# A one-core two-block transformer kernel: the order of work around its norms, its start and its attention heads

## The chip, the core and the metric

The kernel runs on one core of one Trainium2 chip. Its engines are TensorE (PE), VectorE (DVE), ScalarE (ACT), GpSimd (POOL) and SyncE (SP), which issues most of the DMAs. The metric is the device time of one execution in microseconds, as the median of several runs.

## The reference, cut to what matters

One sequence of T = 256 tokens of width 1024 passes through two blocks, all in fp32.

```python
# first block
xn = rmsnorm(x, norm1_g)
h = x + token_mixers(xn)           # w_in (1024 x 7168), RG-LRU scan, convolutions, gates, w_out
t = rmsnorm(h, norm2_g)
q = t @ w_q                        # PEER: 8 heads, two halves of 128 keys each, top 16 of 256 sums
h = h + sum(gate * gelu(u[idx] . t) * v[idx])    # 16384 experts; u and v are 16384 x 1024
x2 = rmsnorm(h, final_g)
# second block, layer 0: differential attention; layer 1: forgetting attention
for i in (0, 1):
    y = attention_i(h)             # 8 differential or 16 forgetting heads
    h = layer_norm(ALPHA * h + y)
    gate, up = split(h @ ffn_w_in) # 2816 each
    f = (silu(conv3(gate)) * up) @ ffn_w_out
    h = layer_norm(ALPHA * h + f)
```

The kernel does not gather experts. It multiplies every token with all 16384 rows of u and of v, and the gates are zero where an expert was not chosen.

## The kernel before, in words

**Products.** TensorE multiplies in a form that takes an fp32 operand rounded to fewer bits. So each operand is split in a high part and a low rest, and each product is made of three (`mm3`, L206 to L209; `add_part`, L231 to L237): high by high, low by high, high by low. Two layouts occur. `proj` gives features by tokens (128x256, 24 products for one weight tile of 128 output features); `add_part` gives tokens by features (128x512), and adds over many weight tiles into four PSUM banks `acc`, one for each pair of token half `tt` and column half `nh`. Four further banks, tag `w`, are handed out by `bank` in turn.

**Weights.** `attn_order` and `ffn_order` write down the order of all weight tiles, 512 KB each. `w_dma` issues their loads on SP's queue into `raw`, `w_split` makes `whi` on ScalarE (L186) and `wlo` on VectorE (L187). They run ahead of their use by as many tiles as there are buffers.

**Order.** The code is written engine by engine in the order of a program, and a scheduler reorders each engine's instructions by its own estimate. `pin` keeps an instruction in program order, and `paced` and `queued` let an instruction be placed only behind a given other one (for `paced`, the latest weight split).

**Stages.** At the start, x is transposed for the sums of squares of norm1 (`x_turn`, `x_sums`) and the first projections `xa` are made of x times the gain, `xgh` and `xgl`; the norm's factor `rB` is multiplied in afterwards. Then follow the input projections (`vb`, `bb`, `cb`, `gx`, `ga`, `ma`, `mb`), with the recurrence `lru_ops` on VectorE and `tables`, which makes rotary tables and one lambda, and the output product `wo`. `finish` runs the last weight tiles for one quarter of the output after another and calls `after` for each quarter.

**Turns.** Where a norm ends, the tokens-by-features result must be turned to features by tokens. `turned` transposes four 128x128 squares into one bank `tq`, copies the high part out on ScalarE and the rest on VectorE. For norm2 and norm3, `residual` adds the quarter to the residual `hk` (called `Hr` for norm3) on VectorE, multiplies it by the norm's gain (`hg`; for norm3 written into the other half of `Hr`), turns it, and sums squares on ScalarE. For a layer norm, `layer_norm` writes sums `z` and the norm's result into one tile.

**PEER.** `q` projections use norm2's turned result; the choice of the top 16 runs on VectorE while 128 `u` tiles are projected; then 128 `v` tiles are added into `pv`. Behind them the `dpv` products (values) and `dqk` (queries and keys) of differential attention begin with norm3's turned result, `x3h` and `x3l`.

**Attention.** `attention` loops over n from 0 to 7. For each n it projects a query and key tile, and at first one value tile too. `scores` makes a head's scores and softmax, `tp` transposes the probabilities `a` (bank `d1tp` for head 1), `pv_` multiplies them with the values (`do`), and `ot` turns the head's result (`dt`) and splits it into `doh` and `dol`. `wo(m)` adds head m into the output (`dwo`). The last part of `attention` writes the order of the remaining heads by hand.

**FFN.** `ffn` makes for each column c a gate product `fg` and an up product `fu`, a convolution and SiLU `fy` on ScalarE and VectorE, and later the output product `fo`. Four of the up products are made early in the other layout (`ul`) and only transposed in the loop.

Of the kernel before, what the change touches and what calls it, by code (L numbers as in the profile page):

```python
# [21 lines left out]
T = 256  # L22
# [9 lines left out]
NW = 3  # L32
# [3 lines left out]
LEAD = 4  # L36
NEG = -1.0e30
# [20 lines left out]
def kernel(  # L58
# [57 lines left out]
    def attn_order(tag, vt, qk, wo):  # L116
        for k in range(LEAD):
            order.append(((tag + "v", k), vt[k]))
        for n in range(8):
            order.append(((tag + "q", n), qk[n]))  # L120
            order.append(((tag + "k", n), qk[8 + n]))
            if LEAD + n < 8:
                order.append(((tag + "v", LEAD + n), vt[LEAD + n]))
        for n in range(8):
            order.append(((tag + "o", n), wo[n]))

    def ffn_order(i):
        for j in range(4):
            order.append((("fl%d" % i, j), [ff_in[i, NF:NF + 4, :, (2 * j + kk) * 128:(2 * j + kk + 1) * 128]
                                            for kk in range(2)]))  # L130
        for c in range(NF):
            order.append((("fg%d" % i, c), ff_in[i, c]))
            if c >= 4:
                order.append((("fu%d" % i, c), ff_in[i, NF + c]))
# [219 lines left out]
    with tc.tile_pool(name="b1", bufs=1) as b1, tc.tile_pool(name="w1", bufs=1) as w1:  # L354
# [15 lines left out]
        w_dma(4)  # L370
# [10 lines left out]
        def scaled(c):  # L381
            act.activation(xgh[:, c, :], x[:, c, :], AF.Copy, scale=P_("norm1_g", c))
            dve.scalar_tensor_tensor(xgl[:, c, :], x[:, c, :], P_("norm1_g", c), xgh[:, c, :].bitcast(F32),
                                     op0=OP.mult, op1=OP.subtract)
# [16 lines left out]
        x_turn(0)  # L401
        for c in range(2):
            scaled(c)
        w_split(1)
        for c in range(2, 4):
            scaled(c)
        x_turn(1)
        x_sums(0)
        for c in range(4, KC):
            scaled(c)  # L410
        w_split(2)
        x_sums(1)
# [9 lines left out]
        XG = 3  # L422
        pss = {}

        def xa_proj(c):
            W = weight(("in", c))
            pss[c] = bank([128, T], f"xa{c}")
            proj(pss[c], W, xgh, xgl)

        for c in range(XG):  # L430
            xa_proj(c)
# [3 lines left out]
        for c in range(8):  # L435
            if c >= XG:
                xa_proj(c)
            ps = pss.pop(c)
            dve.tensor_tensor(xa[:, c, :], ps, rB, op=OP.mult)
# [4 lines left out]
                                     op0=OP.mult, op1=OP.subtract)  # L444

# [29 lines left out]
        nl = b1.tile([128, 8], F32, name="nlam8")  # L475
        ab = b1.tile([128, 8], F32, name="lamabs")
        zz = b1.tile([128, 8], F32, name="zz")
        dve.tensor_scalar(nl, lamc, -1.0, None, op0=OP.mult)
        dve.tensor_tensor(ab, nl, lamc, op=OP.max)
        act.activation(zz, ab, AF.Exp, scale=-1.0)  # L480
        series_log1p(sp4, zz, [128, 8], b1, "sp")
        dve.scalar_tensor_tensor(sp4, nl, 0.0, sp4, op0=OP.max, op1=OP.add)
        dve.tensor_scalar(sp8, sp4, -8.0, None, op0=OP.mult)
        dve.tensor_scalar(sp4, sp4, 4.0, None, op0=OP.mult)
        dve.tensor_scalar(g8, P_("subln"), 1.0 - LAM_INIT, None, op0=OP.mult)
# [90 lines left out]
        tables()  # L576
# [29 lines left out]
        g2 = full("g2", tag="xch").rearrange("p a b -> p (a b)")[:, 0:D]  # L606
        row_bcast(g2, "norm2_g")
        hg = full("hg", tag="xnh").rearrange("p a b -> p (a b)").rearrange("p (t d) -> p t d", t=2)

        def residual(hk, xk, hg, grow, acc, ss, junk, xh, xl):  # L610


            def after(tt, nh):
                ns = slice(nh * 512, nh * 512 + 512)
# [7 lines left out]
        junk = full("junk2", tag="yb").rearrange("p a b -> p (a b)")[:, 0:512]  # L622
        finish(acc, tail, residual(hk, xk, hg, g2, acc, ss2, junk, hgh, hgl))
        nc.sync.dma_start(hdram, hk.rearrange("p a b -> p (a b)"))
        st["behind"] = []
# [3 lines left out]
    with pctx:  # L629
# [256 lines left out]
        finish(acc, tail, residual(hk, hk, hg, g3, acc, ss3, junk, xh, xl))  # L886
# [6 lines left out]
    with ExitStack() as b2ctx:  # L893
# [15 lines left out]
        def layer_norm(acc, tail, h, li, n, rows_, last=False):  # L909
# [3 lines left out]
            z = tokens("z" + name)  # L913
# [12 lines left out]
            def after(tt, nh):  # L926
                ns, nt = slice(nh * 512, nh * 512 + 512), slice(nh, nh + 1)
                pin(dve.scalar_tensor_tensor(z[:, tt, ns], h[:, tt, ns], ALPHA, acc[2 * tt + nh], op0=OP.mult,
                                             op1=OP.add, accum_out=s[:, tt, nt]))
# [3 lines left out]
                if nh == 0:  # L933
                    return
                t1 = slice(tt, tt + 1)
                pin(dve.tensor_scalar(nm[:, t1], m[:, tt, 0:1], m[:, tt, 1:2], 0.5, op0=OP.add, op1=OP.mult))
                for j in range(2):
                    js = slice(j * 512, j * 512 + 512)
                    pin(dve.scalar_tensor_tensor(z[:, tt, js], z[:, tt, js], nm[:, t1], rows_[0][:, js], op0=OP.add,
                                                 op1=OP.mult))  # L940
                    if j == 0:
# [479 lines left out]
```

## Time and profile before

| What | Value |
|---|---|
| Runs | 1758.74, 1761.19, 1765.67 us; median 1761.19 us |
| Profiled execution | 1761.87 us |
| Its span | 1760.1 us |
| TensorE busy | 1693.4 us (96%) |
| TensorE weight loads busy | 1541.5 us (88%) |
| VectorE busy | 1219.4 us (69%) |
| ScalarE busy | 884.4 us (50%) |
| Chain that ended last | TensorE 79%, VectorE 10%, ScalarE 4% |

The span is what the trace covers; the execution's own time has 1.8 us around it. A high busy share says that an engine is the one to look at, not that it was busy all along at its peak: the rows further down show where it waited, and for what, and at which clock it ran.

### The profile page before, as it was taken

How to read it: one execution, taken by the hardware profiler on the slowest of the kernel's cores; microseconds unless marked ns; L12 is line 12 of the kernel's file. 1: busy time of each engine (PE TensorE's matmuls, PEld its weight loads, DVE VectorE, ACT ScalarE, POOL GpSimd, SP SyncE). 2: the span in 40 equal slices, each digit the busy share in tenths (PEclk: the TensorE clock that was granted, in tenths of full speed). 3: DMA queues.
4: the chain of work that ended last, by engine and by line, in shares of the span. 5: the costliest groups of instructions: out<-in, count | busy, mean ns of one | idle time of the engine just before them, and what ended most of it. 6: DMA issues, size and time to landing. Idle time of an engine off the chain costs nothing.

```text
span 1760.1 us, 30460 instructions
## 1 busy us (share of the span) xinstructions
PE 1693.4 (96%) x11917; PEld 1541.5 (88%) x11917; DVE 1219.4 (69%) x2332; ACT 884.4 (50%) x1498; POOL 128.4 (7%) x104
## 2 busy tenths in 40 slices
PE   7999799999999999999999998988999999999998
PEld 7999699899999999887788886886899979989997
DVE  8868589985477776888855554785766665566665
ACT  6684455444433334445444443564645446555453
POOL 2023010430000000000000000241000000000000
PEclk9999899999999999999999999999999999999999
DMA  7646446455544445446565553741755545347551
GB/s 239 191 158 200 147 144 216 156 176 184 180 156 156 155 156 163 159 159 194 168 216 192 191 192 112 235 132 48 231 188 186 186 147 163 99 134 219 184 186 55
DMA packets 90719, 297.17 MB, mean 169 GB/s; under 512 B 9216, under 2 KB 20560, under 8 KB 89808
## 3 DMA queue, kind: packets, MB, share of 16 engines
q1 hardware_dynamic: 89520, 294.71, 52.0%
q8 instruction: 93, 1.52, 0.4%
q10 hardware_dynamic: 1056, 0.52, 0.1%
q14 instruction: 50, 0.41, 0.1%
HBM read 289.92 MB, written 3.19 MB: 167 GB/s over the span
## 4 chain that ended last, share of the span: by engine, by line
PE 79%; DVE 10%; ACT 4%; issue 2%; DMA 2%; POOL 1%; POOLq 0%; ACTq 0%; SPq 0%; DVEq 0%
PE pv L235 20%; PE ff L235 7%; PE u L207 5%; PE u L208 5%; PE u L209 5%; DVE wlo L187 3%; PE fg L207 2%; PE fg L209 2%; PE fg L208 2%; PE fu L209 2%; PE fu L207 2%; PE fu L208 2%; PE g L815 2%; PE g L816 2%; PE fwo L235 1%
## 5 line engine op out<-in xcount | busy, mean ns | idle before, releaser
L187 DVE TENSOR_TENSOR wlo<-raw,whi 128x1024 fp32r<-128x1024 f32 x384 | 474.9, 1238 | 222.6 <-ACT whi L186 215.7
L186 ACT ACTIVATE whi<-raw 128x1024 fp32r<-128x1024 f32 x384 | 405.5, 1058 | 263.2 <-PE pv L235 118.9
L187 DVE TENSOR_TENSOR W<-raw,W 128x1024 fp32r<-128x1024 f32 x150 | 185.2, 1237 | 124.1 <-ACT W L186 123.7
L208 PE MATMUL u<-xn2h,wlo 128*128 128x256 f32 x928 | 262.8, 283 | 6.0 <-DVE wlo L187 6.0
L207 PE MATMUL u<-xn2h,whi 128*128 128x256 f32 x928 | 264.4, 285 | 0.0
L209 PE MATMUL u<-xn2l,whi 128*128 128x256 f32 x928 | 261.8, 282 | 0.0
L186 ACT ACTIVATE W<-raw 128x1024 fp32r<-128x1024 f32 x150 | 158.4, 1060 | 171.4 <-PE pv L235 67.8
L208 PEld LDWEIGHTS u<-xn2h,wlo 128*128 128x128 f32 x928 | 175.6, 189 | 7.7 <-DVE wlo L187 7.7
L207 PEld LDWEIGHTS u<-xn2h,whi 128*128 128x128 f32 x928 | 176.0, 190 | 0.0
L209 PEld LDWEIGHTS u<-xn2l,whi 128*128 128x128 f32 x928 | 175.4, 189 | 0.0
L835 ACT ACTIVATE H<-u 128x256 f32<-128x256 f32 x128 | 49.2, 384 | 224.4 <-PE u L209 224.4
L235 PE MATMUL pv<-W,ph 128*128 128x512 f32 x416 | 116.3, 391 | 0.0
L235 PE MATMUL pv<-whi,pl 128*128 128x512 f32 x304 | 96.5, 397 | 0.7 <-DVE pl L318 0.7
L235 PE MATMUL pv<-wlo,ph 128*128 128x512 f32 x304 | 95.5, 394 | 0.0
L235 PE MATMUL pv<-whi,ph 128*128 128x512 f32 x304 | 92.3, 402 | 0.0
L235 PEld LDWEIGHTS pv<-W,ph 128*128 128x128 f32 x416 | 77.7, 188 | 16.2
L816 PE MATMUL g<-al,eb 128*128 128x64 f16 x512 | 70.8, 239 | 0.0
L815 PE MATMUL g<-ah,eb 128*128 128x64 f16 x512 | 70.8, 239 | 0.0
L235 PEld LDWEIGHTS pv<-wlo,ph 128*128 128x128 f32 x304 | 57.1, 188 | 13.5
L235 PEld LDWEIGHTS pv<-whi,pl 128*128 128x128 f32 x304 | 56.8, 189 | 13.9 <-DVE pl L318 1.1
L815 PEld LDWEIGHTS <-eb 128*128 128x128 f16 x512 | 56.2, 117 | 11.4 <-issue 6.0
L235 PEld LDWEIGHTS pv<-whi,ph 128*128 128x128 f32 x304 | 55.8, 190 | 10.9
(840 smaller groups left out, 4397.0 us busy)
## 6 DMA issues: line engine op xcount, KB each, us to landing
raw<-in_uT_dram SPq DMA_DIRECT2D x128, 512.0 KB, 3.6
raw<-in_v_dram SPq DMA_DIRECT2D x128, 512.0 KB, 4.2
raw<-in_ff_in_dram SPq DMA_DIRECT2D x80, 512.0 KB, 3.8
raw<-in_w_in_dram SPq DMA_DIRECT2D x56, 512.0 KB, 4.3
raw<-in_ff_out_dram SPq DMA_DIRECT2D x44, 512.0 KB, 3.8
raw<-in_w_q_dram SPq DMA_DIRECT2D x16, 512.0 KB, 3.5
raw<-in_qkw_dram SPq DMA_DIRECT2D x16, 512.0 KB, 4.2
raw<-in_f_qk_dram SPq DMA_DIRECT2D x16, 512.0 KB, 4.2
```

The costliest lines, as they stand in the source:

```text
L186: st["hi"] = act.activation(hi, r, AF.Copy).ins
L187: st["lo"] = dve.tensor_tensor(lo, r, hi.bitcast(F32), op=OP.subtract).ins
L207: pe.matmul(o, w[0], x[0], start=start, stop=False, skip_group_check=True)
L208: pe.matmul(o, w[1], x[0], start=False, stop=False, skip_group_check=True)
L209: pe.matmul(o, w[0], x[1], start=False, stop=stop, skip_group_check=True)
L235: i = pe.matmul(acc[2 * tt + nh], x_[:, ts], w_[:, nh * 512:nh * 512 + 512], start=f, stop=l, skip_group_check=True)
L815: pe.matmul(gps[:, t, :], eb[:, g, :, j], ah[:, g, :, j], start=True, stop=False)
L816: pe.matmul(gps[:, t, :], eb[:, g, :, j], al[:, g, :, j], start=False, stop=True)
L835: act.activation(Hs[i // 32][:, o:o + T], ps, AF.Gelu_apprx_tanh)
```

## The change

The change has eight parts.

1. The start. Weight 0 is the first load on SP; two of x's three loads go to ScalarE's queue. Weight 0 is split in two halves, the first ahead of all. The first four `xa` are copied out of their banks by ScalarE at once, and VectorE multiplies them with `rB` later.
2. `tables` and the series for the recurrence's lambda are paced by the weight splits.
3. Norm2. The gain is no longer multiplied into `hg`. All four quarters of `hk` are added first, `hk` itself is transposed into four banks `tp` by feature pair, and the gain is applied as ScalarE's scale (`hgh`) and VectorE's scalar (`hgl`). The last two `wo` tiles go by token half, then quarter.
4. Norm3. `after3` holds a quarter's turn back until the next quarter has been added and multiplied.
5. `layer_norm`: the next token half's first sums come before the turns of this half; the result `y` is written over the old residual `h`. In the last one, the second copy out of a bank is VectorE's.
6. Differential attention takes its value tiles one n later (`VN`), `tp` behind the value tile, and the hand-written tail runs `values` and `turns` so that a head's turn stands ahead of the output product of the head before.
7. Norm3's factor for the residual `h3` goes into the layer norm's scalar (`r3a`) in place of a multiplication of `h3`.
8. The four early up products of an FFN are those of columns 2, 7, 12 and 17 (`UL`), no longer 0 to 3.

```diff
+VN = {"d": 1, "f": 0}
+UL = (2, 7, 12, 17)
...
-        nc.sync.dma_start(x[:, 0:2, :], xT[:, 0:2, :])
+        w_dma(1)
+        nc.scalar.dma_start(x[:, 0:2, :], xT[:, 0:2, :])
         nc.sync.dma_start(PAR, par)
-        nc.sync.dma_start(x[:, 2:4, :], xT[:, 2:4, :])
-        w_dma(1)
+        nc.scalar.dma_start(x[:, 2:4, :], xT[:, 2:4, :])
         nc.sync.dma_start(x[:, 4:8, :], xT[:, 4:8, :])
...
+        def first_split(h):
+            hs = slice(h * 512, h * 512 + 512)
+            i = pin(act.activation(hi[:, hs], r[:, hs], AF.Copy))
+            j = pin(dve.tensor_tensor(lo[:, hs], r[:, hs], hi[:, hs].bitcast(F32), op=OP.subtract))
+            st["hi"], st["lo"] = i.ins, j.ins
...
+        XG = 4
         for c in range(XG):
-            xa_proj(c)
+            ps = bank([128, T], f"xa{c}")
+            proj(ps, weight(("in", c)), xgh, xgl)
+            act.activation(xa[:, c, :], ps, AF.Copy)
...
+        for c in range(XG):
+            dve.tensor_tensor(xa[:, c, :], xa[:, c, :], rB, op=OP.mult)
...
-        tables()
+        with paced():
+            tables()
...
-                pin(dve.tensor_tensor(hk[:, tt, ns], xk[:, tt, ns], acc[2 * tt + nh], op=OP.add))
-                pin(dve.tensor_tensor(hg[:, tt, ns], hk[:, tt, ns], grow[:, ns], op=OP.mult))
-                turned(hg, tt, nh, xh, xl)
-                act.activation(junk, hk[:, tt, ns], AF.Square, accum_out=ss[:, tt, nh:nh + 1])
-            return after
+        def after2(tt, nh):
+            ns = slice(nh * 512, nh * 512 + 512)
+            dve.tensor_tensor(hk[:, tt, ns], xk[:, tt, ns], acc[2 * tt + nh], op=OP.add)
+            act.activation(junk, hk[:, tt, ns], AF.Square, accum_out=ss2[:, tt, nh:nh + 1])
+            if tt == 0 and nh == 0:
+                return
+            for c in range(8) if tt == 0 else range(4 * nh, 4 * nh + 4):
+                pe.transpose(tp[c // 2][:, c % 2, tt * 128:tt * 128 + 128], hk[:, tt, c * 128:c * 128 + 128], ident)
...
+        for c in range(8):
+            src = tp[c // 2][:, c % 2, :]
+            act.activation(hgh[:, c, :], src, AF.Copy, scale=P_("norm2_g", c))
+            dve.scalar_tensor_tensor(hgl[:, c, :], src, P_("norm2_g", c), hgh[:, c, :].bitcast(F32), op0=OP.mult,
+                                     op1=OP.subtract)
...
+        def after3(tt, nh):
+            ns = slice(nh * 512, nh * 512 + 512)
+            pin(dve.tensor_tensor(hk[:, tt, ns], hk[:, tt, ns], acc[2 * tt + nh], op=OP.add))
+            pin(dve.tensor_tensor(hg[:, tt, ns], hk[:, tt, ns], g3[:, ns], op=OP.mult))
+            late.append((tt, nh))
+            if len(late) == 2:
+                turned(hg, *late.pop(0), xh, xl)
+            act.activation(junk, hk[:, tt, ns], AF.Square, accum_out=ss3[:, tt, nh:nh + 1])
...
                 if nh == 0:
+                    if tt:
+                        turns(0)
                     return
...
+                gain(1)
+                offset(0)
+                offset(1)
+                if tt:
+                    turns(1)
...
-                if c < 4:
+                if c in UL:
...
+                if n >= 2:
+                    tp(n - 2)
                 if n >= 1:
                     scores(n - 1)
-                if n >= 5:
-                    pv_(n - 5, V, own(2))
-                if n >= 6:
-                    o[n - 6] = ot(n - 6, own(3))
+                if n >= v1 + 2:
+                    pv_(n - v1 - 2, V, own(2))
+                if n >= v1 + 3:
+                    o[n - v1 - 3] = ot(n - v1 - 3, own(3))
...
+            values(1)
+            turns(1)
             wo(0)
             tp(6)
-            pv_(4, V, bank)
+            values(1)
             wo(1)
             scores(7)
-            o[3] = ot(3, bank)
-            pv_(5, V, bank)
+            turns(1)
+            values(1)
             wo(2)
             tp(7)
-            o[4] = ot(4, bank)
-            pv_(6, V, bank)
-            pv_(7, V, bank)
-            o[5] = ot(5, bank)
+            turns(1)
+            values(8)
+            turns(1)
             wo(3)
-            o[6] = ot(6, bank)
-            o[7] = ot(7, bank)
+            turns(8)
...
+        dve.tensor_scalar(r3a, r3, ALPHA, None, op0=OP.mult)
...
-            if n == 2:
-                with tc.issue_after(i.ins):
-                    for tt in range(2):
-                        dve.tensor_scalar(h3[:, tt, :], h3[:, tt, :], r3[:, tt:tt + 1], None, op0=OP.mult)
```

The scheduler decides where these instructions land. Line numbers in the changed kernel are larger: `hk` at L615 becomes L627, the split at L187 becomes L189.

On VectorE at the end of the first block, before: two splits of `q` weights, and then add, gain product and low part, one quarter after another.

```order
L187 TENSOR_TENSOR wlo_2545<-raw_2462,whi_2544 128x1024
L187 TENSOR_TENSOR wlo_2551<-raw_2486,whi_2550 128x1024
L615 TENSOR_TENSOR hk<-M_91,wo_2129 128x512
L616 TENSOR_TENSOR hg<-hk,g_2541 128x512
L300 TENSOR_TENSOR hgl<-tq,hgh 128x4x128
L615 TENSOR_TENSOR hk<-M_91,wo_2130 128x512
L616 TENSOR_TENSOR hg<-hk,g_2541 128x512
L300 TENSOR_TENSOR hgl<-tq,hgh 128x4x128
```

After, at the same place, with `tp` the four banks of transposes:

```order
L189 TENSOR_TENSOR wlo_2552<-raw_2468,whi_2551 128x1024
L627 TENSOR_TENSOR hk<-M_91,wo_2135 128x512
L627 TENSOR_TENSOR hk<-M_91,wo_2136 128x512
L627 TENSOR_TENSOR hk<-M_91,wo_2137 128x512
L627 TENSOR_TENSOR hk<-M_91,wo_2138 128x512
L189 TENSOR_TENSOR wlo_2558<-raw_2492,whi_2557 128x1024
L643 SCALAR_TENSOR_TENSOR hgl<-tp_2547,par_sb,hgh 128x256
L643 SCALAR_TENSOR_TENSOR hgl<-tp_2548,par_sb,hgh 128x256
```

One split has moved behind the four adds, the gain products are gone, and the low parts come behind all adds.

On VectorE at the end of PEER, before: the second `Hr` row of each pair is the product with the gain, `x3l` the low part of a turned quarter.

```order
L615 TENSOR_TENSOR Hr<-Hr,pv_8604 128x512
L616 TENSOR_TENSOR Hr<-Hr 128x512
L300 TENSOR_TENSOR x3l<-tq,x3h 128x4x128
L615 TENSOR_TENSOR Hr<-Hr,pv_8605 128x512
L616 TENSOR_TENSOR Hr<-Hr 128x512
```

After:

```order
L909 TENSOR_TENSOR Hr<-Hr,pv_8611 128x512
L910 TENSOR_TENSOR Hr<-Hr 128x512
L909 TENSOR_TENSOR Hr<-Hr,pv_8612 128x512
L910 TENSOR_TENSOR Hr<-Hr 128x512
L302 TENSOR_TENSOR x3l<-tq,x3h 128x4x128
```

The first `x3l` has moved behind the second quarter's add and product; the others follow in the same way, one quarter late.

On ScalarE where the `ma` projections begin, before (`sa` is the sigmoid of `ma`):

```order
L186 ACTIVATE whi_1847<-raw_1706 128x1024
L582 ACT_TABLE_LOAD
L582 ACTIVATE sa_1878<-ma_1853 128x256
L186 ACTIVATE whi_1881<-raw_1745 128x1024
L582 ACTIVATE sa_1912<-ma_1887 128x256
L186 ACTIVATE whi_1915<-raw_1784 128x1024
L582 ACTIVATE sa_1946<-ma_1921 128x256
```

After, where L530 is the exponential for the lambda in `tables`:

```order
L188 ACTIVATE whi_1853<-raw_1712 128x1024
L597 ACT_TABLE_LOAD
L597 ACTIVATE sa_1884<-ma_1859 128x256
L188 ACTIVATE whi_1887<-raw_1751 128x1024
L530 ACT_TABLE_LOAD
L530 ACTIVATE ls<-ls 128x2
L597 ACT_TABLE_LOAD
L597 ACTIVATE sa_1918<-ma_1893 128x256
L188 ACTIVATE whi_1921<-raw_1790 128x1024
```

Two table loads and an exponential have come between the first two sigmoids; ahead of the sigmoids of `ma` 5 and 6, the sines of `tables` come in the same way.

## Rows read from the trace of the kernel before

**Rows 1.** The page: busy us, share of the span, instructions, by engine.

```profile
PE 1693.4 (96%) x11917; PEld 1541.5 (88%) x11917; DVE 1219.4 (69%) x2332; ACT 884.4 (50%) x1498; POOL 128.4 (7%) x104
```

**Rows 2.** TensorE's waits: tile it worked for, releaser: us, times, longest.

```profile
PE tq L296 <- DVE hg L616: 12.2, 4, 4.0
PE u L208 <- DVE wlo L187: 6.0, 8, 1.8
...
PE xa L207 <- ACT rB L434: 3.2, 1, 3.2
PE dwo L235 <- ACT doh L1215: 3.1, 2, 2.5
PE tq L296 <- DVE Hr L616: 2.8, 1, 2.8
...
PE d1tp L1138 <- ACT whi L186: 2.3, 1, 2.3
PE fg L207 <- DVE fy L1002: 2.1, 2, 1.1
PE dwo L235 <- DVE dol L1216: 1.9, 1, 1.9
PE ma L208 <- DVE wlo L187: 1.6, 2, 0.9
...
PE tq L296 <- DVE zln L950: 1.3, 3, 0.7
```

**Rows 3.** Busy us of PE, PEld, DVE, ACT, POOL by stretch; clock, DMA, GB/s.

```profile
0.00:20.00 20.00, 13.23 (x92) 12.36 (x92) 14.82 (x54) 11.82 (x24) 3.38 (x7) 1.00 0.79 286
...
140.00:160.00 20.00, 18.40 (x154) 17.99 (x153) 17.14 (x22) 9.03 (x14) 9.47 (x9) 1.00 0.59 202
200.00:220.00 20.00, 9.87 (x38) 6.58 (x37) 8.85 (x14) 6.20 (x12) 0.00 (x0) 0.74 0.24 79
220.00:240.00 20.00, 17.69 (x133) 17.69 (x134) 12.51 (x35) 10.13 (x23) 5.63 (x7) 0.83 0.34 119
240.00:260.00 20.00, 20.00 (x172) 20.00 (x171) 20.00 (x83) 12.49 (x28) 2.65 (x4) 1.00 0.50 162
```

**Rows 4.** Timeline, 205 to 224 us: start, duration, instruction, idle before it.

```profile
206.36 0.39 PE L235 MATMUL wo<-wlo,mh 128*128 128x512 f32 x1
207.00 2.36 DVE L187 TENSOR_TENSOR wlo<-raw,whi 128x1024 fp32r<-128x1024 f32 x2 [5.24 <-ACT whi L186]
...
209.28 0.68 DVE L615 TENSOR_TENSOR hk<-M,wo 128x512 f32<-128x512 f32 x1
...
210.74 1.12 PE L296 MATMUL tq<-ident,hg 128*128 128x128 f32 x4 [3.99 <-DVE hg L616]
...
223.08 0.56 PE L207 MATMUL q<-hgh,whi 128*128 128x256 f32 x1
```

**Rows 5.** Groups by form, first 60 us: count, busy us, mean ns.

```profile
L382 ACT ACTIVATE xgh<-M,par_sb 128x256 fp32r<-128x256 f32 x8 | 3.5, 496 | 0.0
...
L503 DVE SCALAR_TENSOR_TENSOR ang<-kq,ang 128x256 f32<-128x256 f32 x3 | 1.3, 424 | 0.0
```

**Rows 6.** Busy time by stretch at the end of PEER.

```profile
1088.00:1092.00 4.00, 4.00 (x10) 2.91 (x10) 1.88 (x5) 0.72 (x2) 0.70 (x1) 0.50 0.40 164
...
1100.00:1104.00 4.00, 4.00 (x24) 4.00 (x23) 2.49 (x3) 0.00 (x0) 0.27 (x2) 0.58 0.99 336
...
sum 32.00, PE 25.98 PEld 21.01 DVE 12.64 ACT 8.98 POOL 4.37; mean PE 3.25 PEld 2.63 DVE 1.58 ACT 1.12 POOL 0.55
```

**Rows 7.** Busy time by stretch in differential attention.

```profile
1172.00:1204.00 32.00, 26.53 (x153) 21.87 (x152) 21.64 (x54) 19.69 (x65) 7.64 (x8) 0.89 0.33 99
...
sum 110.00, PE 97.85 PEld 84.81 DVE 81.10 ACT 71.62 POOL 35.54; mean PE 24.46 PEld 21.20 DVE 20.27 ACT 17.91 POOL 8.88
```

**Rows 8.** ScalarE's timeline at the first product of `ma`.

```profile
139.41 1.28 ACT L582 ACT_TABLE_LOAD   x1
140.71 0.39 ACT L582 ACTIVATE sa<-ma 128x256 f32<-128x256 f32 x1
```

More of the change, by code (lines that the diff above doesn't have):

```diff
@@ L132, in ffn_order @@
             order.append((("fg%d" % i, c), ff_in[i, c]))
-            if c >= 4:
+            if c not in UL:
                 order.append((("fu%d" % i, c), ff_in[i, NF + c]))
@@ L575 @@
             act.activation(sg[:, c, :], ps, AF.Gelu_apprx_tanh)
-        tables()
+        with paced():
+            tables()
         for c in range(8):
@@ L621 @@
-        tail = [(weight(("wo", k)), (mh[:, k, :], ml[:, k, :])) for k in (6, 7)]
-        junk = full("junk2", tag="yb").rearrange("p a b -> p (a b)")[:, 0:512]
-        finish(acc, tail, residual(hk, xk, hg, g2, acc, ss2, junk, hgh, hgl))
+        tp = [pacc.tile([128, 2, T], F32, tag=f"acc{j}", name=f"tp{j}") if j < 2 else
+              bank([128, 2, T], f"tp{j}") for j in range(4)]
+        junk = full("junk2", tag="yb").rearrange("p a b -> p (a b)")[:, 0:512]
+        def after2(tt, nh):
[6 more added lines that the diff above has]
+                pe.transpose(tp[c // 2][:, c % 2, tt * 128:tt * 128 + 128], hk[:, tt, c * 128:c * 128 + 128], ident)
@@ new lines @@
+        tail = [(weight(("wo", k)), (mh[:, k, :], ml[:, k, :])) for k in (6, 7)]
+        for tt, halves in ((0, (0, 1)), (1, (0,)), (1, (1,))):
+            for j, (W, p) in enumerate(tail):
+                add_part(acc, W, p, tt, halves, False, j == 1)
+            for nh in halves:
+                after2(tt, nh)
+        for c in range(8):
[3 more added lines that the diff above has]
+                                     op1=OP.subtract)
@@ L884 @@
         tail = [(weight(("v", i), i == 125), gated(i)) for i in range(125, 128)]
-        finish(acc, tail, residual(hk, hk, hg, g3, acc, ss3, junk, xh, xl))
+        def after3(tt, nh):
[6 more added lines that the diff above has]
+            act.activation(junk, hk[:, tt, ns], AF.Square, accum_out=ss3[:, tt, nh:nh + 1])
+        late = []
+        finish(acc, tail, after3)
+        turned(hg, *late.pop(), xh, xl)
         nc.sync.dma_start(h3dram, Hr[:, 2048:4096])
@@ L948, in after, with gain @@
-                for j in range(2):
-                    js = slice(j * 512, j * 512 + 512)
-                    pin(dve.scalar_tensor_tensor(z[:, tt, js], z[:, tt, js], r[:, t1], rows_[1][:, js], op0=OP.mult,
-                                                 op1=OP.add))
-                    if not last and j:
-                        turned(z, tt, 0, xh, xl)
-                        turned(z, tt, 1, xh, xl)
+                t1, js = slice(tt, tt + 1), [slice(0, 512), slice(512, 1024)]
+                def gain(j):
+                    pin(dve.scalar_tensor_tensor(y[:, tt, js[j]], z[:, tt, js[j]], nm[:, t1], rows_[0][:, js[j]],
+                                                 op0=OP.add, op1=OP.mult))
@@ new lines, in after, with turns @@
+                gain(0)
+                pin(dve.tensor_scalar(v[:, t1], q[:, tt, 0:1], q[:, tt, 1:2], 1.0 / D, op0=OP.add, op1=OP.mult))
+                pin(dve.scalar_tensor_tensor(v[:, t1], v[:, t1], 1e-5, d[:, t1], op0=OP.add, op1=OP.add))
+                pool.tensor_tensor(r[:, t1], v[:, t1], nhalf[:, t1], op=OP.pow)
+                gain(1)
[3 more added lines that the diff above has]
+                    turns(1)
+            def turns(tt):
+                for j in range(2):
```

137 lines of the change are left out of this document (68 added, 69 removed).

## The prediction, made before the changed kernel ran

> **What bounds the kernel now.** The first view is the page's busy times: TensorE is busy for 96% of the span, VectorE for 69% and ScalarE for half [rows 1]. The change removes no TensorE product, so what it can win is TensorE's idle time (1760.1 − 1693.4 = 66.7 us) and the time in which it ran at half its clock. The second view, TensorE's waits, says where the idle time lies: 12.2 us in four waits for `hg` between the first block's last product and the PEER stage, and after that in pieces of 1 to 6 us [rows 2]. The third, busy time by stretch, says what else was slow there: 200 to 220 us has TensorE busy for 9.87 of 20 us at a mean clock of 0.74, and the next stretch is at 0.83 [rows 3]. The reader is to see that VectorE and ScalarE were idle there too (8.85 and 6.20 us busy): no engine was full, the three waited for each other in turn.
>
> **C, the end of the first block and norm2.** The timeline gives the chain [rows 4]. The last product of `wo` starts at 206.36 and lasts 0.39, so it ends at 206.75. Then VectorE does two weight splits (2.36), adds a half of `hk` (0.68), multiplies it by the gain, and only at 210.74 do four transposes run. Three more such rounds follow, and the first `q` product starts at 223.08, 16.3 us after `wo`. The work that has to lie in between is sixteen transposes, 4 × 0.56 = 2.2 us (four took 1.12 at half clock). The row of 220 to 240 us with its clock of 0.83 is 20 × 0.17 × 2 = 6.8 us at half clock, so up to 226.8; the `q` products from 223.08 to there took 3.7 us and would have taken half: 1.85 lost. So C now costs 16.3 − 2.2 + 1.85 = 15.9 us above its products.
> After the change no gain multiply lies between, the four adds stand behind each other on VectorE, and all sixteen transposes go into four banks. One split stands ahead of the adds; its buffer comes free when weight 6 has been used, 12 products before the end. A 128x256 product takes 0.116 us (172 in 20 us [rows 3]) and one of 512 columns twice that, so that is 2.8 us before, and with ScalarE's part and VectorE's 1.18 (half of 2.36) it ends about when `wo` does. The first two adds then end 1 us behind `wo`, the first eight transposes at 2.1, the other two adds beside them, and the first gain copy on ScalarE starts at 2.5. ScalarE has eight copies of 0.50 (the same form as `xgh` [rows 5]) and between them two squares over 512 columns, which I put at 0.8 against 0.50 for 256: 5.6 us, so the last ends at 8.1, and VectorE's part 0.5 behind it. Since the first two `q` weights are taken in turns, their 48 products run while the copies arrive, and end about 9 us behind `wo`, or 11 if the clock falls in the short wait. The pure work is 2.2 + 5.6 = 7.8 us, so 1.2 to 3.2 us stay of 15.9: a gain of 12.7 to 14.7. If `q` waits for all copies instead, it ends at 8.6 + 5.6 + 1.4 (clock) = 15.6, and the gain is 8.1. I take **12**, 8 to 14.
>
> **D, the end of PEER and norm3.** In 1076 to 1108 us TensorE was busy 25.98 of 32 us: 6.0 idle. Two of the stretches show the clock at 0.50 and 0.58, and with the others the loss is 4.6 us (4 × (0.50 + 0.42) = 3.7, and 0.9 from those left out) [rows 6]. Together 10.6. The reason is one wait of 2.8 for the scaled `Hr` [rows 2]: its add and multiply stood behind a low part `x3l` on VectorE, which needs the transposes of the half before. The change puts each half's transposes behind the next half's sums, so VectorE works through add and multiply without that wait, and 24 products of `dpv` (5.6 us) stand ahead of the last eight transposes. What stays is the wait for the first high and low part, under 1 us. I take **9.7**, 7 to 10.6.
>
> **E, differential attention.** From 1108 to 1218 us TensorE was busy 97.85 of 110, and 1172 to 1204 alone ran at a clock of 0.89, 3.5 us lost [rows 7]: 15.6 us in all. The change aims at three waits: 2.3 for `d1tp` (the row names a split, but the probabilities were late too: VectorE had the residual's scaling by r3 ahead of them, which is gone, folded into the norm's scalar); 3.1 and 1.9 for `doh` and `dol`, the split of a head directly ahead of its `dwo` products, which now get a head's distance [rows 2]. They are 7.3, and their part of the clock loss 3. Against that, v tiles move one head later, so one head more of values and turns is left for the tail. I count half: **5**, −3 (two more waits of 2.5 in the tail, and the scaling's alone gone) to 12.
>
> **The norms and the FFN's start.** `fg` waited 2.1 us for the convolution `fy` where the first four up projections are ready-made, so no products lie between; the change spreads them over columns 2, 7, 12 and 17. The turns behind the norms waited 1.3 [rows 2]; the next half's sums now stand ahead of them. **3**, 1 to 3.4. The last norm's end has no cover either way, its second half's sums come behind one copy more: **−0.5**, 0 to −1.
>
> **A, the start.** `xa` waited 3.2 us for `rB`, since its banks were held until the norm was known [rows 2]. ScalarE now empties them at once. Against it stands that x's tiles come on ScalarE's queue beside weight 0, and the first 20 us already moved 286 GB/s with the DMA engines busy at 0.79 [rows 3]: the parameters and x come later as weight 0 comes earlier, and ScalarE gets four copies more. I take **2**, 0 to 4.5.
> The Trainium skill (DMA: Bandwidth & Descriptors, Issuing engines are not separate DMA queues) says that transfers of all queues share the engines, and only the issue time is saved; by that nothing is won from the second queue. The share of 0.79 agrees, and the sum with 0 for A would be 2 us later.
>
> **B, what is moved behind the gates.** The rotary tables and the lambda series were done in the first 60 us [rows 5]. Now they come, paced by the splits, when `ma` is projected. VectorE is 17.14 of 20 us busy there and TensorE waits 1.6 for its splits [rows 3, 2]. About 17 operations come in, the longest kind 0.42; at 0.3 on the mean, about 5 us. ScalarE gets five table loads more of 1.28 [rows 8], 6.4 us, in a stretch where it was 9.03 of 20 us busy. The splits ahead of TensorE absorb some: **−3**, −0.5 to −5.
>
> **Sum.** 12 + 9.7 + 5 + 3 − 0.5 + 2 − 3 = 28.2 us. The profiled execution took 1761.87, 0.7 above the median of the runs; 1761.19 − 28.2 = **1733**. With all lower bounds 8 + 7 − 3 + 1 − 1 + 0 − 5 = 7 us are won (1754), with all upper ones 44 (1717).
>
> **Rivals.**
> *VectorE takes C's gain back.* From 240 to 260 us VectorE is busy 20.00 of 20 (topk), and TensorE waits 6.0 for the splits of `u` behind it [rows 3, 2]. If that stretch has its own length from a start that doesn't move, C's 12 are lost: 1745. Against it: topk waits for `q`, and VectorE had 11 and 7.5 us idle in the two stretches before, so its start should move too. 0.13.
> *The clock and the copies.* `q` runs behind the copies at half clock, and D's second half too: C 8, D 7, so 1733 + 6.7 = 1740. For it: every wait of some 2.5 us here was followed by half clock. 0.12.
> *Each table load stops the splits.* Each of three places has two loads and a function of 0.4 at 3 us; if TensorE waits for two thirds of 9 us and VectorE's 5 in full, B is −11 and the time 1741. 0.06.
> The Trainium skill (ScalarE: Activation LUTs, What ACT_TABLE_LOAD costs) adds a drain of 1.38 us to each switch; 13.3 us for five, not 6.4. The trace differs: the load begins at 139.41, lasts 1.28, and the next activation starts at 140.71 [rows 8].
> *The scheduler's order at D gives nothing* (the last transposes behind `dpv` only move the wait): D 0, 1743. 0.05.
> *Slower: the heads' chain.* Now E loses 15.6 us, 2 a head. With turns behind `scores` and a head more in the tail, each of eight heads could wait 4.5 us more (one more round between the engines, as norm2's take (223.08 − 210.74) / 3 = 4.1 each [rows 4]). Then E is −36, the sum −13, the time 1774. It decides from 2.9 a head (23.2 / 8). Against it: the turn gets more products ahead of it, not fewer, and VectorE has 29 us idle in the 110. 0.03.
> My forecast has 0.61.
>
> **Range and chances.** A measurement here can tell about 0.5%, 8.8 us. All cases but the last lie below 1752.4. Two of the rivals together, or the lower bounds, reach it: same 0.06, slower 0.03, faster 0.91. The range leaves out the heads' chain and the far ends: 1717 to 1748.
>
> **What would show it.** C: the first `q` under 5 us behind the last `wo`, no `tq` wait for `hg`, and the stretch behind it at a clock over 0.9. D: no wait for `Hr` over 1 us, clock near 1. A: no wait for `rB`. B: TensorE's wait for `ma`'s splits up from 1.6 to 3 to 6. E: no wait for `doh` or `dol` over 1. The waits for `u`'s splits stay near 6; 15 or more would speak for the first rival. I am wrong if 230 to 360 us takes as long as before after an earlier start, or if heads' waits add up to over 17 us.

## The result, and the profile after

The changed kernel took 1731.45 us (median of four runs, 1728.83 to 1732.92) beside 1760.57 us of the kernel before: a ratio of 0.9828, with a 95% interval of 0.9804 to 0.9853. That is 29.1 us less, where 28.2 were forecast. The profiled execution took 1732.03 us, and its span is 1730.1.

First the page's busy times of the changed kernel, against [rows 1]. TensorE does the same work; it is busy 9.5 us less, since fewer products ran at half clock, and its idle time fell from 66.7 to 1730.1 − 1683.9 = 46.2 us.

```profile
PE 1683.9 (97%) x11917; PEld 1537.0 (89%) x11917; DVE 1218.5 (70%) x2334; ACT 892.2 (52%) x1510; POOL 128.7 (7%) x104
```

Next, TensorE's waits in the changed kernel, against [rows 2].

```profile
PE xps L396 <- DMA M<-in_xT_dram: 5.9, 1, 5.9
PE u L210 <- DVE wlo L189: 5.3, 7, 1.8
...
PE d5tp L1196 <- DVE a L1231: 3.5, 1, 3.5
PE d2tp L1196 <- ACT W L188: 2.4, 1, 2.4
PE ul L1021 <- ACT xhln L301: 2.4, 4, 0.9
PE ma L210 <- DVE wlo L189: 1.8, 2, 1.3
PE q L209 <- ACT hgh L642: 1.7, 2, 1.5
PE d1tp L1196 <- ACT whi L188: 1.6, 1, 1.6
PE d6tp L1196 <- ACT W L188: 1.4, 1, 1.4
...
PE dwo L237 <- DVE dol L1269: 1.1, 1, 1.1
...
PE mb L210 <- DVE wlo L189: 0.8, 1, 0.8
...
PE wo L237 <- ACT mh L319: 0.4, 1, 0.4
...
PE wo L237 <- DVE ml L320: 0.3, 1, 0.3
```

The waits for `hg` (12.2), for `rB` (3.2), for `Hr` (2.8), for `doh` (3.1) and of `fg` for `fy` (2.1) are gone. New or longer are the waits for the probabilities of heads 2, 5 and 6 and for the first tiles of x (`xps`), and `ul`, the first product behind a layer norm, waits longer.

At the end of the first block the stretches now read as follows, against 9.87 and 17.69 us busy at clocks of 0.74 and 0.83 in [rows 3] (the first row is the stretch of the `ma` projections, for term B below):

```profile
140.00:160.00 20.00, 18.18 (x149) 17.58 (x148) 19.86 (x37) 13.08 (x18) 8.49 (x8) 1.00 0.51 164
200.00:220.00 20.00, 18.09 (x107) 15.62 (x106) 11.48 (x23) 10.52 (x26) 3.19 (x4) 0.91 0.38 133
220.00:240.00 20.00, 20.00 (x173) 20.00 (x172) 20.00 (x72) 14.01 (x33) 5.62 (x6) 1.00 0.50 159
```

The timeline shows the chain of [rows 4] as it is now. The last `wo` product starts at 205.94, the four adds run in one piece, and the first `q` product starts 3.1 us behind the last `wo` product's start, where it was 16.7.

```profile
205.63 2.47 DVE L627 TENSOR_TENSOR hk<-M,wo 128x512 f32<-128x512 f32 x4
...
205.94 0.39 PE L237 MATMUL wo<-wlo,mh 128*128 128x512 f32 x1
...
206.97 1.85 PE L632 MATMUL tp<-ident,hk 128*128 128x128 f32 x14 [0.15 <-DVE hk L627]
...
209.02 0.39 PE L209 MATMUL q<-hgh,whi 128*128 128x256 f32 x1 [0.20 <-ACT hgh L642]
...
209.48 1.19 ACT L642 ACTIVATE hgh<-tp,par_sb 128x256 fp32r<-128x256 f32 x3
...
210.55 0.64 ACT L628 ACTIVATE M<-hk 128x512 f32<-128x512 f32 x1
...
211.16 1.21 ACT L642 ACTIVATE hgh<-tp,par_sb 128x256 fp32r<-128x256 f32 x3
...
211.70 0.39 PE L209 MATMUL q<-hgh,whi 128*128 128x256 f32 x1 [1.50 <-ACT hgh L642]
```

At the end of PEER, the first row below has the 32 us from just ahead of the last `pv` products on, against 25.98 of 32 us busy in [rows 6]:

```profile
1064.00:1096.00 32.00, 31.98 (x202) 27.90 (x201) 21.05 (x31) 15.38 (x23) 11.55 (x11) 1.00 0.59 217
...
1128.00:1160.00 32.00, 26.09 (x196) 24.39 (x196) 25.12 (x51) 21.59 (x61) 13.63 (x8) 0.92 0.42 132
```

The first row has next to no idle time (0.02 us) and the full clock. The second, in differential attention, still has 5.9 us idle and a clock of 0.92.

To see where the time came from, the program is cut at the first and last start of the products of some tiles, which the view of a tile gives. The table has the stretches that differ, in us, for the kernel before, for two profiles of the changed kernel, and for the runs below that undo a part in that stretch.

| Stretch | Before | After | After again | With the part undone |
|---|---|---|---|---|
| start to first `ma` | 136.0 | 133.4 | 133.5 | 134.7 (start of before), 132.9 and 133.1 (tables early) |
| first `ma` to last `wo` | 70.4 | 72.5 | 72.5 | 69.6 and 69.7 (tables early), 74.2 (norm2 of before) |
| last `wo` to first `u` | 71.8 | 60.1 | 58.5 | 70.7 (norm2 of before) |
| first `u` to last `u` | 407.8 | 408.9 | 407.7 | |
| last `pv` to last `dwo` | 148.9 | 133.4 | 133.8 | 142.3 (norm3 at once), 137.6 (attention of before) |
| first `fg` to first `fqk` | 198.4 | 195.8 | 195.9 | 197.3 (`ul` first) |
| last `fwo` to last `fg` | 179.7 | 178.5 | 178.4 | 180.5 (`ul` first) |
| last `fg` to the end | 25.7 | 26.2 | 26.2 | 27.3 (norm2 of before) |

### The profile page after: what moved, and what is told of

Read it like the earlier page. It is cut to its first block, busy times and chain, and to the rows that moved or that the text cites. A ratio compares the mean times of both kernels' runs of the same rounds, so it can differ in the third digit from the quotient of the medians.

```text
span 1730.1 us, 30470 instructions
## 1 busy us (share of the span) xinstructions
PE 1683.9 (97%) x11917; PEld 1537.0 (89%) x11917; DVE 1218.5 (70%) x2334; ACT 892.2 (52%) x1510; POOL 128.7 (7%) x104
## 4 chain that ended last, share of the span: by engine, by line
PE 80%; DVE 9%; ACT 5%; DMA 3%; issue 2%; POOL 1%; POOLq 0%; ACTq 0%; SPq 0%; DVEq 0%
PE pv L237 21%; PE ff L237 6%; PE u L209 6%; PE u L210 6%; PE u L211 6%; DVE wlo L189 3%; PE fg L209 2%; PE fg L210 2%; PE fg L211 2%; PE fu L209 2%; PE fu L211 2%; PE fu L210 2%; PE g L835 2%; PE g L836 2%; PE ul L1021 1%
## 5 line engine op out<-in xcount | busy, mean ns | idle before, releaser
L189 DVE TENSOR_TENSOR wlo<-raw,whi 128x1024 fp32r<-128x1024 f32 x383 | 472.3, 1234 | 209.0 <-ACT whi L188 205.7
L189 DVE TENSOR_TENSOR W<-raw,W 128x1024 fp32r<-128x1024 f32 x150 | 186.2, 1244 | 115.2 <-ACT W L188 113.9
```

The lines of the kernel that those rows point to most:

```text
L189: st["lo"] = dve.tensor_tensor(lo, r, hi.bitcast(F32), op=OP.subtract).ins
```

## The experiments

Twelve runs follow: ten edits of the changed kernel, one of them run twice, and the changed kernel again. Runs of one kernel lay 2 to 7 us apart, so small parts are read from the stretches. Those with no edit in them mostly repeat within some tenths; the one from the last `wo` to the first `u` product has two lengths, told of at the end, and the one from the last `pv` to the last `dwo` product differs by up to 2 us. So a part of 1 or 2 us there, read from one profile, is not clear of chance.

**Norm3's turns at once.** Each quarter is turned as soon as it is multiplied, as before.

```diff
-            if len(late) == 2:
+            if len(late) == 1:
...
-        turned(hg, *late.pop(), xh, xl)
```

> The changed kernel with norm3's quarters turned at once, as before; everything else as changed. My theory: the held turn is worth the 9.7 us of D, so about 1741 us, with a wait of 2.5 to 3 us for Hr again, and the stretch from the last pv to the last dwo product at about 143 us (133.4 in the changed kernel, 148.9 before). Rival: differential attention alone shortened that stretch, since it waited for later heads anyway; then under 3 us are lost and it stays below 137.

It took 1739.17 us, ratio 0.9874 (0.9857 to 0.9891). TensorE's waits have the old row again:

```profile
PE tq L298 <- DVE Hr L910: 2.8, 1, 2.8
```

The stretch from the last `pv` to the last `dwo` product took 142.3 us; in the eight profiles whose attention and norm3 are as changed it took 132.7 to 133.8 in seven and 131.9 in one. So D is worth about 8.9 us (8.5 to 10.4 against those eight). That is more than the 2.8 us of the wait: TensorE's idle time in the stretch is 17.6 us in place of 10.8, and the clock falls again, to 0.62 and 0.68 in two pieces of four microseconds (1075 to 1079 and 1087 to 1091). The rival that attention alone made the stretch shorter falls.

**Norm2 of before.** `after2` and the copies by column are replaced by `residual` and `finish` of before.

```diff
-        for tt, halves in ((0, (0, 1)), (1, (0,)), (1, (1,))):
-            for j, (W, p) in enumerate(tail):
-                add_part(acc, W, p, tt, halves, False, j == 1)
-            for nh in halves:
-                after2(tt, nh)
...
+        finish(acc, tail, residual(hk, xk, hg, g2, acc, ss2, junk, hgh, hgl))
```

> The changed kernel with norm2 of the kernel before (gain multiply, each quarter added and turned before the next). My theory: C is worth 11 to 12 us, and the stretches behind it do not give it back: about 1743 us, the last wo to the first u product 71 to 72 us (60.1 in the changed kernel). Rival (VectorE's topk sets that stretch): the time from there to the last u product is shorter by as much as C is longer, and under 5 us are lost in all.

It took 1743.77 us, ratio 0.9899 (0.9882 to 0.9915), 12.9 us more than the changed kernel's ratio gives on the same kernel before (1761.24 × 0.9828 = 1730.9). The wait for `hg` is the one of before, to the tenth:

```profile
PE tq L298 <- DVE hg L631: 12.2, 4, 4.0
```

From the last `wo` to the first `u` product it took 70.7 us, and 407.9 from there to the last `u`, as in every other run (407.3 to 408.9). So the stretch in which VectorE is full has its own length, but it starts when `q` does: nothing of C is given back there. The rest of the 12.9 us lies mostly in two other stretches: the one from the first `ma` to the last `wo` product, which holds norm2's order of the last `wo` tiles, took 74.2 us in place of 72.5, and the end 27.3 in place of 26.2, for which no run shows a cause.

**Norm2 with held turns.** As the run before, but with each turn behind the next quarter's add and product, so that what is new in norm2 is split in two.

```diff
-                turned(hg, tt, nh, xh, xl)
+                held.append((tt, nh))
+                if len(held) == 2:
+                    turned(hg, *held.pop(0), xh, xl)
```

> As the run with norm2 of before, but each quarter's turn is held back until the next quarter is added and multiplied, as the change does in norm3; the gain multiply stays. If the serial turn alone was the cost: VectorE's four adds and products of 1.3 us follow each other, 5.4 us, the last turn about 2 us later, so q starts about 9 us behind wo in place of 16.3 and 2.8, and about 6 to 7 of C's 12 come back: 1737 us. Rival: the late gain with all copies in columns is what counts (the q products run beside the copies); then under 3 us come back and the time stays near 1742.

It took 1738.44 us, ratio 0.9867 (0.9851 to 0.9883). The wait for `hg` fell to 6.5 us, of which 4.0 is the first:

```profile
PE tq L298 <- DVE hg L631: 6.5, 4, 4.0
```

From the last `wo` to the first `u` product it took 65.8 us. So 4.9 us of C come from the hold alone, and the other 5.7 to 7.3 us (65.8 − 60.1 or 58.5) from adds without gain products, one split less ahead of them, and copies by column that let `q` begin; no run takes these three apart. The 6 to 7 us that were expected of the hold were too many, the rival's under 3 too few.

**Tables early.** The `paced` around the series and around `tables` is taken out.

```diff
-        with paced():
-            tables()
+        tables()
```

> The changed kernel with tables and the lambda series not paced, so that the scheduler may put them early as before. My theory: pacing costs 2.1 us at ma (its splits wait, five table loads more), so about 1729 to 1730 us, if the start doesn't lose as much: VectorE is full there (18.7 of 20 us from 20 to 40). Rival: the pacing makes room at the start, and without it xa waits and 2 us or more are lost: 1733 to 1735.

It took 1727.39 us, ratio 0.9808 (0.9791 to 0.9824). From the first `ma` to the last `wo` it took 69.6 us in place of 72.5, and of the waits in that stretch only one row is left:

```profile
PE ma L210 <- DVE wlo L189: 1.6, 2, 0.9
```

The first `ma` started at 132.9 us, where it started at 132.8 to 133.6 in the runs that have the changed start and the pacing. So the pacing costs 2.9 us and gives nothing back at the changed start.

**The start of before**, loads, splits and held banks.

```diff
-        XG = 4
-        for c in range(XG):
-            ps = bank([128, T], f"xa{c}")
-            proj(ps, weight(("in", c)), xgh, xgl)
-            act.activation(xa[:, c, :], ps, AF.Copy)
+        XG = 3
...
+        for c in range(XG):
+            xa_proj(c)
```

> The changed kernel with the start of before (order of the first loads, no halves, banks of xa held for rB). My theory: A is worth 2 to 3 us: 1733.5 to 1734.5 us, the wait of xa for rB is 3 us again and the first vb product starts at 36.5 to 37.5 us (33.9 in the changed kernel). Rival (loads share the engines, nothing won): 1731.5.

It took 1732.15 us, ratio 0.984 (0.9822 to 0.9857): not to be told from the changed kernel. The first `vb` product started at 36.4 us, just ahead of the 36.5 to 37.5 expected, but the wait for `rB` was not 3 us:

```profile
PE xps L396 <- DMA M<-in_xT_dram: 6.0, 2, 3.7
...
PE xa L209 <- ACT whi L188: 1.3, 1, 1.3
...
PE xa L209 <- ACT rB L436: 0.9, 1, 0.9
```

The one other difference from the kernel before at this place is that the tables are paced, and the wait is 2.3 us shorter than in [rows 2]. The first `ma` product started at 134.7 us, 1.2 to 1.3 behind the two profiles of the changed kernel and 1.3 ahead of the kernel before. So with the tables paced the new start is worth about 1.3 us, and taking the tables out of the old start as much. The two do not simply add: in the runs with the tables early the new start alone brings the first `ma` to 132.9 and 133.1, which is 3.1 and 2.9 us ahead of the kernel before.

**The attention of before**: value tiles early, the old loop and tail, the residual scaled on VectorE.

```diff
-VN = {"d": 1, "f": 0}
+VN = {"d": 0, "f": 0}
...
-            values(1)
-            turns(1)
+            pv_(3, V, bank)
+            o[2] = ot(2, bank)
             wo(0)
...
+                        dve.tensor_scalar(h3[:, tt, :], h3[:, tt, :], r3[:, tt:tt + 1], None, op0=OP.mult)
```

> The changed kernel with differential and forgetting attention of before: value tiles one n earlier, the tail of before, the residual scaled by r3 on VectorE. My theory: E is worth 5 to 6 us (15.5 of D and E together, less the 8.9 that undoing D cost): 1737 us, the stretch from the last pv to the last dwo product 139 us (133.4 in the changed kernel), doh and dol wait 5 us again. Rival: the heads wait for later things in any case and the waits only move; then under 2 us are lost.

It took 1732.94 us, ratio 0.9844 (0.9828 to 0.9861). The stretch took 137.6 us, so E is worth 4.2 against 133.4 (3.8 to 5.7 against the eight profiles); by the median of the whole time the difference is 1.3 us (1732.94 less 1761.99 × 0.9828), inside the interval. Of the stretch TensorE was idle for 12.3 us here and 10.8 in the changed kernel, so most of the 4.2 is not idle time. The three waits of the prediction are back:

```profile
PE d1tp L1181 <- ACT whi L188: 3.2, 1, 3.2
PE dwo L237 <- ACT doh L1257: 3.1, 2, 2.5
...
PE dwo L237 <- DVE dol L1258: 1.9, 1, 1.9
```

**The residual scaled again**, with the tail and value tiles as changed.

```diff
+            if n == 2:
+                with tc.issue_after(i.ins):
+                    for tt in range(2):
+                        dve.tensor_scalar(h3[:, tt, :], h3[:, tt, :], r3[:, tt:tt + 1], None, op0=OP.mult)
```

> The changed kernel with only the scaling of the residual by r3 put back on VectorE (two instructions of 1.4 us in all, behind the third head's rotation). If the probabilities of heads 1 and 2 wait for it: 1 to 3 us lost, all between 1096 and 1160 us. Rival: VectorE has room there (25 of 32 us), under 0.5 us.

It took 1732.32 us, ratio 0.9835 (0.9819 to 0.9852), and the stretch 136.2 us: 2.8 more than as changed, and 2.4 more than the longest of the eight profiles. Head 1 waits 4.3 us in place of 1.6, and `doh` waits more than in the kernel before, in spite of the new tail:

```profile
PE dwo L237 <- ACT doh L1270: 5.0, 4, 3.2
...
PE d1tp L1194 <- DVE a L1233: 4.3, 1, 4.3
```

**Value tiles early**, with the new loop and no scaling. The calls of the hand-written tail follow from `VN`: with the value tiles early, `values` and `turns` come to the very order that the kernel before has written out. So this run takes back the later value tile and the tail's new order together.

```diff
-VN = {"d": 1, "f": 0}
+VN = {"d": 0, "f": 0}
```

> The changed kernel with the value tiles of differential attention one head earlier again, tail and scaling as changed. If the later tile covers the first heads' softmax: the waits for d1tp and d2tp grow by 2 to 3 us, 1733 to 1735 us. Rival: the head that the later tile leaves for the tail costs as much (waits for d5tp and d6tp, 3.5 and 1.4, shrink): no difference over 1 us.

It took 1732.17 us, ratio 0.9832 (0.9815 to 0.9848), and the stretch 134.3 us, 0.5 more than the longest of the eight profiles. So the rival, no difference over 1 us, held. The waits for heads 5 and 6 are gone, as it said, and those for `doh` and `dol` are the ones of the kernel before:

```profile
PE dwo L237 <- ACT doh L1268: 3.1, 2, 2.5
...
PE dwo L237 <- DVE dol L1269: 1.9, 1, 1.9
...
PE d1tp L1196 <- ACT whi L188: 1.8, 1, 1.8
```

**Only the scaling gone**: the loop, the tail and the value tiles of before, the residual not scaled. As the tail is the same, it differs from the run before only in where `tp` stands in the loop, and in one head's bank.

```diff
-            values(1)
-            turns(1)
+            pv_(3, V, bank)
+            o[2] = ot(2, bank)
             wo(0)
```

> The changed kernel with the loop and the tail of attention of before and value tiles one n earlier; of E's three edits only one stays, the scaling of the residual gone from VectorE. The stretch from the last pv to the last dwo product took 133.4 us with all three, 137.6 with none, 134.3 with tail and scaling edit, 136.2 with tail and value edit. Theory: the scaling edit alone carries most of E: 134 to 135 us here. Rival: the tail's order is needed for it: 136.5 or more.

It took 1732.32 us, ratio 0.9834 (0.9818 to 0.985), and the stretch 136.0 us. That lies between the theory (134 to 135) and the rival (136.5 or more), so neither came true. Taken one by one from the old attention on, the missing scaling gives 1.6 of E's 4.2 us (137.6 − 136.0), the place of `tp` 1.7 (to 134.3), the later value tile with its tail 0.9 (to 133.4); put back alone into the changed kernel, the scaling costs 2.8. Each of these is one profile, and profiles with the same attention lie 1.9 us apart. Only the 2.8 is clear of that; how the rest divides stays open.

**The changed kernel again.**

> The changed kernel once more, on the same chip as the three others, to read them against. Expected 1731.5 us, the stretch from the last pv to the last dwo product between 132 and 134 us, from the last wo to the last u product between 466 and 469 (the range that the same code showed in seven profiles).

It took 1730.11 us, ratio 0.9818 (0.9801 to 0.9835). The stretch from the last `wo` to the last `u` product took 466.2 us, inside what was expected.

**Tables early again**, on the same chip.

> The changed kernel with tables and series not paced, once more and beside the changed kernel on the same chip: 3 to 4 us faster than that, near 1728 us, if the pacing is the loss; if the earlier difference was chance or the chip, under 1 us.

It took 1727.28 us, ratio 0.9805 (0.9789 to 0.9822): 2.8 us under the changed kernel beside it, just short of the 3 to 4 expected. The two intervals overlap, so the whole times alone don't decide; the stretch does, with 69.7 us against 72.5, as in the first run. This version is the fastest of all.

**The early up products at columns 0 to 3.**

```diff
-UL = (2, 7, 12, 17)
+UL = (0, 1, 2, 3)
...
-            order.append((("fl%d" % i, j), [ff_in[i, NF + 2:NF + 18:5, :, (2 * j + kk) * 128:(2 * j + kk + 1) * 128]
+            order.append((("fl%d" % i, j), [ff_in[i, NF:NF + 4, :, (2 * j + kk) * 128:(2 * j + kk + 1) * 128]
```

> The changed kernel with the early up products at columns 0 to 3 again, in both FFNs. My theory: fg waits for fy 2 us again, 1 us in each FFN, and the time is about 2 us longer (the stretch from the first fg to the first fqk product 197 us, 195.8 in the changed kernel, 198.4 before). Rival: the gain there is the norms' alone, and the stretch stays at 195.8.

It took 1732.33 us, ratio 0.9839 (0.9823 to 0.9855), 2.2 us more than the changed kernel beside it, and the old wait is back:

```profile
PE fg L209 <- DVE fy L1045: 2.1, 2, 1.2
```

The two stretches that hold an FFN's columns are 1.4 and 2.1 us longer. So the spread columns are worth about 3.5 us by these stretches and 2.2 by the whole time, and the rival falls. The wait itself is 2.1 us; for what goes beyond it no row names a cause.

## Why the prediction was right

The time was right to 1.6 us, and the terms were right one by one, mostly in their size. For E and B the size was partly luck: E is half of what was aimed at, and B is work of some 11 us less an amount that the prediction only guessed.

**C** was set at 12. The stretch behind `wo` became 11.7 us shorter in one profile and 13.3 in the other. Up to `q` the chain ran as it was worked out: `q` began 2.7 us behind the end of `wo`, 2.5 plus one copy having been forecast, and then waited once more, for 1.5 us. The prediction had the products run while the copies arrive. They did not follow copy by copy: the next three copies were done by 210.67, and TensorE went on only behind the start of the fifth, which stands behind a square (210.55 and 211.16 in the timeline above). Why the three were not enough the trace does not show.

**D** was set at 9.7 and measured 8.9. No wait stayed at the norm itself. D and E, each undone alone, come to 13.1 us; their common stretch became 15.5 us shorter, so some 2.4 us come only with both or from chance.

**E** was set at 5 and measured 4.2, but its steps fared unevenly. Of the three waits of 7.3 us only the one for `doh` went wholly; head 1 still waits 1.6 of 2.3 us and `dol` 1.1 of 1.9, over the 1 that was to show success. The prediction put the tail's order down as a gain and the later value tiles as a cost. They are one edit, since the tail's order follows from `VN`: with the value tiles early the order is the old one, and the waits for `doh` and `dol` were 3.1 and 1.9 us as ever. With the tiles later they shrank, and heads 2, 5 and 6 waited 2.4, 3.5 and 1.4 us. So the edits move waits from one head to another, and the sum of the waits that go is not the gain.

**The norms and the FFN** were set at 3. The two stretches with FFN columns became 3.8 us shorter and the one ahead of the first `fg` 0.3 longer. The spread columns carry it with about 3.5. The layer norms' own edit shows no gain: the 1.3 us that `tq` waited are gone, but `ul`, the next product, now waits 2.4 us for the turned high part. In the kernel before that was:

```profile
PE ul L979 <- ACT xhln L299: 0.5, 2, 0.3
```

So the wait moved one product on. From the last `dwo` to the first `fg` product, the stretch of the first layer norm, it took 15.5 us before, 15.5 and 15.6 in the two runs that have the new layer norm and the old scaling of the residual, and 15.7 to 15.8 in all others. So the new order of the norm gives nothing there, and the 0.3 us lost go with the folded scaling, which the prediction counted as a gain alone.

**The end** lost 0.5, the size that was forecast. No run undoes that edit, and edits far from it moved this stretch between 25.9 and 27.3 us, so the cause is not shown.

**A** was set at 2, and the first `ma` started 2.6 us sooner. The wait for `rB` is gone, as said. The start's edits carry it: with the tables early they gave 3.1 and 2.9 us, and the pacing adds nothing to that. Had the old start stayed, the tables' leaving alone would have won 1.3, which the prediction counted at nothing. What the second queue gives by itself no run shows. As the prediction feared, x came later: the wait for its first tiles is 5.9 us now, where the kernel before had these two rows, of which the second is gone:

```profile
PE xps L394 <- DMA M<-in_xT_dram: 4.3, 2, 3.9
...
PE xa L207 <- ACT whi L186: 2.5, 1, 2.5
```

**B** was set at −3 and measured −2.9. The place was only half right: the wait for `ma`'s splits is 1.8, not the 3 to 6 that was to show it, and the loss lies a little later, in waits of `mb` (0.8) and `wo` (0.4 and 0.3). Against the one row of 1.6 with the tables early these make 1.7 of the 2.9 us; for the rest no row names a wait. VectorE was full from 140 to 160 us, 19.86 of 20, where it was 17.14 in [rows 3]. Had the table loads each a drain of 1.38 us, as the Trainium skill states (ScalarE: Activation LUTs, What ACT_TABLE_LOAD costs), ScalarE would show it. The trace differs. In the changed kernel, too, an activation follows 0.02 us behind a load of 1.28, and the load begins 0.01 us behind the instruction ahead of it (158.59 + 1.06, then 159.66):

```profile
157.01 1.28 ACT L597 ACT_TABLE_LOAD   x1
158.31 0.38 ACT L597 ACTIVATE sa<-ma 128x256 f32<-128x256 f32 x1
158.59 1.06 ACT L188 ACTIVATE whi<-raw 128x1024 fp32r<-128x1024 f32 x1
159.66 1.28 ACT L522 ACT_TABLE_LOAD   x1
160.96 0.42 ACT L522 ACTIVATE rC<-kq 128x256 f32<-128x256 f32 x1
```

**The rivals.** VectorE did not take C's gain back (the run with norm2 of before). The clock did fall behind the copies in five of eleven profiles, at a price of 1.6 us, not 4. That every wait of some 2.5 us was followed by half clock does not hold in the kernel before either: behind the 3.2 us for `rB` it stayed at 1.00 (20 to 40 us). The table loads did not stop the splits for long: B stayed at −2.9, not −11. The order at D did what it says. The heads' chain did become a new wait, with 3.5 us for one head, far from 4.5 us for each. The 4.1 us a round taken for it from norm2 were too many: its rounds start at 210.74, 214.59, 218.43 and 222.31, 3.9 us apart.

## What to carry to other kernels

Where a busy engine waits and no other engine is full, look for a chain that goes around the engines once for each piece; put all pieces of one engine's part behind each other, and only then hand on. Here that gave some 21 of 29 us at two norms. Holding back each turn by one piece is the small edit that brings much of it (4.9 us at norm2, 8.9 at norm3).

A wait that leaves the list is worth its length only if nothing else was nearly as late: price it by the length of its stretch, with the edit undone, and hold the difference against the spread of that stretch in profiles that share its code. Work that hides for nothing in one place (the tables at the start) is not to be moved into a stretch where the same engine is full.

## What was not expected of the hardware

The same program with the same waits did not always run at the same clock. Behind the wait of 1.5 us for the copies, two profiles of the changed kernel show this for the same four microseconds:

```profile
208.00:212.00 4.00, 2.29 (x15) 1.59 (x14) 3.55 (x9) 4.00 (x13) 0.97 (x2) 1.00 0.87 317
212.00:216.00 4.00, 4.00 (x24) 4.00 (x23) 1.35 (x5) 1.12 (x4) 2.22 (x3) 0.61 0.32 121
```

```profile
208.00:212.00 4.00, 2.30 (x16) 1.59 (x14) 3.56 (x9) 4.00 (x13) 0.91 (x2) 1.00 0.87 321
212.00:216.00 4.00, 4.00 (x35) 4.00 (x35) 2.17 (x6) 1.19 (x4) 2.29 (x3) 1.00 0.32 123
```

In the first the clock was at its half level, 1.2 GHz, for most of the stretch and 24 products ran, in the second it stayed full and 35 ran, with the same 2.3 us busy in the four microseconds before. It shows in the stretch from the last `wo` to the first `u` product, too: the eleven profiles with the new norm2 took 58.5 to 59.0 us in six and 60.0 to 60.5 in five. All five had a clock of 0.57 to 0.61 in one of the four-microsecond pieces behind the wait; the six had 1.00 throughout. The Trainium skill (TensorE: Matmul & The Clock Gate, What's actually happening) says that the point at which the clock changes is not tied to the program's start and differs between runs. These profiles agree that it differs; what it hangs on they do not show. So a wait of this length costs half clock in some executions and not in others.
